# Moving start-up memsets and reordering the first loads in a one-core biased-attention kernel

## The chip, the cores and the metric

The kernel runs on one core of one Trainium2 chip. The metric is device time in microseconds (us) of one execution; lower is better. "Span" is the profiled part of an execution, in most runs some 1.8 us shorter than the time. Engines: PE is TensorE's matmul side (its weight loads are shown as PEld), DVE is VectorE, ACT is ScalarE, POOL is GpSimd, SP is SyncE.

## The reference

```
q, k, v: (4, 8, 1024, 64) float32;  bias: (1, 1, 1024, 1024) float32
scores = q @ k.T / sqrt(64) + bias
out    = softmax(scores) @ v            # (4, 8, 1024, 64) float32
```

The 32 heads are worked on in 16 pairs. The kernel computes S transposed on PE, exp on ACT, multiplies by exp(bias) on VectorE, and multiplies by V on PE. A column of ones beside V makes the same product deliver the row sums.

## The kernel before

The change touches only the start and two constants of the planner, a small model inside the kernel's builder that fixes each engine's instruction order. At the start, q and k of pair 0 arrive as float32 on the queues of SP and ACT, are cast to bf16, transposed on PE and copied into `qT0` and `kT0`. `mask` is used only later, by the copies of the other q tiles.

```python
nc.vector.memset(warm[:], 0.0)
nc.vector.memset(zeros[:], 0.0)
...                                                   # loads of kr0, qr0 and half the bias, issued by Pool
for t in range(2):
    nc.vector.memset(qT0[t*D:(t+1)*D, 1-t, :HQ], 0.0)
    for u in range(2):
        nc.vector.memset(mask[t*D:(t+1)*D, u, :], 1.0 if t == u else 0.0)
nc.gpsimd.memset(vall[:, :, :, D:D1], 1.0)            # the ones column: 256 elements per partition, 65 apart
load_v(0); load_qk(1)
...                                                   # second bias half, load_v(1), load_qk(2)
...                                                   # six warm-up matmuls wm on zeros
k_first(0, nc.scalar.copy, nc.scalar.copy, "xb")      # cast, 4 transposes, copy to kT0
c_a = q_first(0, "xa"); c_b = q_first(1, "xb")        # cast on VectorE, 4 transposes each
c_a(); c_b()                                          # copies to qT0 on VectorE
s_fill(0); s_exp(0)                                   # one S bank, first exponential
k_first(2, nc.vector.tensor_copy, nc.vector.tensor_copy, "xa")
s_fill(1); s_exp(1)                                   # two banks; all later groups have three
COLD = 10500; T0 = 6700.0                             # the planner's model of the cold clock and the start
```

The softmax here doesn't subtract the row's maximum and nothing guards it: scores larger than these inputs give would overflow.

Of the kernel before, what the change touches and what calls it, by code (L numbers as in the profile page):

```python
# [15 lines left out]
def kernel(  # L16
# [15 lines left out]
    nc = tc.nc  # L32
    B, H, S, D = q.shape
    P = 128
    NCH = S // P
    D1 = D + 1
    NP = B * H // 2
    scale = 1.0 / (D ** 0.5)
    HQ = S // 2
    QC = NCH // 2  # L40
# [5 lines left out]
    bf_ = bias.rearrange("a b (p c) k -> p (a b c) k", p=P)  # L46
# [12 lines left out]
    btraw = consts.tile([P, NCH, S], BF)  # L59
    eb = consts.tile([P, 2, NCH, HQ], BF)  # L60
    braw = consts.tile([P, 2, HQ], BF)
    mask = consts.tile([P, 2, HQ], BF)
    vall = consts.tile([P, 2 * NP, NCH, D1], BF)
# [8 lines left out]
    def load_qk(pr):  # L72
        qr = raw.tile([P, 2, NCH, D], BF, name="qr")
        kr = raw.tile([P, 2, NCH, D], BF, name="kr")
        nc.gpsimd.dma_start(out=kr.rearrange("p t c d -> p t (c d)"), in_=kf[pr])  # L75
        nc.gpsimd.dma_start(out=qr.rearrange("p t c d -> p t (c d)"), in_=qf[pr])  # L76
        raws[pr] = (qr, kr)

    def load_v(pr):
        for t in range(2):  # L80
            nc.gpsimd.dma_start(out=vall[:, 2 * pr + t, :, :D], in_=vf[pr, :, t])  # L81
# [34 lines left out]
    def e_at(b, n):  # L116
        if b // ET not in etiles:
            etiles[b // ET] = ep.tile([P, ET, HQ], BF, name="E")
        return etiles[b // ET][:, b % ET:b % ET + n, :]
# [3 lines left out]
    def s_fill(g):  # L123
        ps = ps_s.tile([P, 3, HQ], F32, tag="s", name="ps")
        open_ps[("S", g)] = ps
        for j, b in enumerate(slots[g]):
            pr, h, qh, kc = banks[b]
            qT, kT = trs[(pr, 0)], trs[(pr, 1)]
            nc.tensor.matmul(ps[:, j, :], kT[:, kc, :], qT[:, h, qh * HQ:(qh + 1) * HQ],  # L129
                             start=True, stop=b not in late_bias)  # L130
            if b in late_bias:
                nc.tensor.matmul(ps[:, j, :], ident[:], braw[:, late_bias[b], :], start=False, stop=True)

    def s_exp(g):
        n = len(slots[g])
        nc.scalar.activation(e_at(slots[g][0], n), open_ps.pop(("S", g))[:, :n, :], ACTF.Exp, scale=scale)  # L136
# [77 lines left out]
    with tc.manual_schedule():  # L214
# [13 lines left out]
        qT0 = kvp.tile([P, 2, NCH * P], BF, name="qT")  # L228
# [1 line left out]
        nc.gpsimd.dma_start(out=kr0[:, :, QC:, :].rearrange("p t c d -> p t (c d)"), in_=kf[0][:, :, QC * D:])  # L230
        nc.gpsimd.dma_start(out=qr0[:, :, QC:, :].rearrange("p t c d -> p t (c d)"), in_=qf[0][:, :, QC * D:])
        nc.gpsimd.dma_start(out=btraw[:, :QC, :], in_=bf_[:, :QC, :])
        for t in range(2):
            nc.vector.memset(qT0[t * D:(t + 1) * D, 1 - t, :HQ], 0.0)  # L234
            for u in range(2):
                nc.vector.memset(mask[t * D:(t + 1) * D, u, :], 1.0 if t == u else 0.0)  # L236
        nc.gpsimd.memset(vall[:, :, :, D:D1], 1.0)
        load_v(0)
        load_qk(1)
        nc.gpsimd.dma_start(out=btraw[:, QC:, :], in_=bf_[:, QC:, :])  # L240
        load_v(1)
        load_qk(2)

        wm = ps_s.tile([P, 3, HQ], F32, tag="s", name="wm")
        for i in range(6):
# [2 lines left out]
        def k_first(c0, eng_cast, eng_copy, tag):  # L248
            cs = slice(c0, c0 + 2)
            eng_cast(kr0[:, :, cs, :], k0f[:, :, cs, :])  # L250
            px = ps_x.tile([P, 2, P], BF, tag=tag, name="px")
            for c in range(2):
                for t in range(2):
                    nc.tensor.transpose(px[t * D:(t + 1) * D, c, :], kr0[:, t, c0 + c, :], ident[:])  # L254
            eng_copy(kT0[:, cs, :], px[:])
# [14 lines left out]
        s_fill(0)  # L270
        s_exp(0)
        k_first(2, nc.vector.tensor_copy, nc.vector.tensor_copy, "xa")
        for g in range(1, 2):
            s_fill(g)
            s_exp(g)



        COLD = 10500
        EXP, EXP0, QK, AV, TP = 427, 45, 216, 170, 350  # L280
        MUL, COPYQ, COPYK, EVAC, SEM = 600, 650, 420, 620, 80
        order = [("S", g) for g in range(2, NS)]
        for at, x in ((5, (0, 0)), (7, (0, 4)), (11, (1, 0)), (13, (1, 4))):
            order.insert(at, ("B",) + x)
        NO = len(order)
        T0 = 6700.0
        t_act, t_pe, t_dve = T0 + 700, T0, T0 + 500
        filled = []
        act_end = []
        x_free = {"xa": T0 + 500, "xb": T0}  # L290
        x_unit = {}
# [6 lines left out]
        pieces.append((NP, 0, 0))  # L298
        raw_at[NP] = (T0, T0)
        piece_end = {(0, 1, 0): T0, (0, 0, 0): T0}  # L300
        eb_at = {}
        exp_at = {0: T0, 1: T0 + 700, 2: T0 + 700}
        mul_at = {}
# [14 lines left out]
        def pe_cost(t, c):  # L318
            return c * 2 if t < COLD else c

# [4 lines left out]
        def act_end_of(i):  # L325
            if i < 0:
                return T0
            if i < len(act_end):
# [155 lines left out]
        while len(act_end) < NO or av_next < NB or dve_q:  # L484
# [11 lines left out]
            t, who = min(c)  # L496
# [53 lines left out]
```

## Time and profile before

Before the prediction: 252.03 us, median of 3 runs (251.59 to 252.09).

| Reading | Value | View |
|---|---|---|
| ACT busy | 239.0 of 249.9 us | page, part 1 |
| ACT from the first three-bank exponential to the last but a tail | busy all of 9.71 to 243.98 us | busy time by stretch |
| First q cast / second, same shape | 1.50 us / 0.28 us | timeline of VectorE |
| First, second, third, fourth exponential start | 6.77, 8.43, 9.71, 11.07 us | timeline of ACT |

ACT's timeline shows these four exponentials, the third and the fourth merged into one line. Each line gives start, duration, engine, line, operation and, in brackets, the engine's idle time just before it and what ended that:

```profile
6.77 0.60 ACT L136 ACTIVATE E<-ps 128x512 bf16<-128x512 f32 x1 [1.94 <-PE ps L129]
8.43 1.02 ACT L136 ACTIVATE E<-ps 128x1024 bf16<-128x1024 f32 x1 [1.06 <-PE ps L129]
9.71 2.81 ACT L136 ACTIVATE E<-ps 128x1536 bf16<-128x1536 f32 x2 [0.26 <-PE ps L129]
```

Part 1 of the page gives busy time, share of the span and number of instructions of each engine:

```profile
PE 228.8 (92%) x3097; PEld 141.1 (56%) x3152; DVE 221.2 (89%) x380; ACT 239.0 (96%) x180; POOL 54.0 (22%) x73
```

Busy time by stretch: the stretch, its length, then each engine's busy time in the order PE, PEld, DVE, ACT, POOL, then granted clock, DMA share and GB/s:

```profile
9.71:243.98 234.27, 219.90 (x3033) 137.33 (x3089) 213.16 (x360) 234.27 (x174) 45.30 (x58) 1.00 0.64 93
```

The fourth busy time, ACT's, equals the stretch: past 9.71 us ACT is never idle, so what comes earlier only moves the start of a queue of exponentials. The chain of waits says what set that start (start us, duration, what):

```profile
2.94 0.48 DVE mask L236
3.42 0.03 issue
3.46 1.51 DVE qr L258
...
5.01 0.65 PE px L261 x6
...
5.68 0.42 DVE qT L262
...
6.58 0.38 DVE kr L250
...
7.01 0.42 PE px L254 x3
7.43 2.26 PE ps L129 x5
```

The timeline (start, duration, engine, line, operation) puts Pool's memset right inside the slow cast; the line for DVE merges the two casts, 3.46 to 4.95 and 4.88 to 5.15 us:

```profile
3.46 1.70 DVE L258 CAST qr<-q0f 128x256 bf16<-128x256 f32 x2
3.54 1.26 POOL L237 MEMSET vall<- 128x256 bf16 x1
```

At PE's slow clock five S matmuls took 2.31 us, and VectorE was idle for 2.40 us ahead of the copy of K's second half (L102), which is the gap that the prediction counts on:

```profile
7.36 2.31 PE L129 MATMUL ps<-qT,kT 128*128 128x512 bf16 x5
10.16 0.42 DVE L102 COPY kT<-px 128x512 bf16<-128x512 bf16 x1 [2.40 <-PE px L89]
```

### The profile page before, as it was taken

The page shows a single profiled execution, that of the slowest core. Times are in us where ns is not written, and L with a number is a line of the kernel's source. Part 1 is how long each engine was busy: PE and PEld are TensorE (multiplying, and loading weights), DVE is VectorE, ACT ScalarE, POOL GpSimd, SP SyncE. Part 2 cuts the span into 40 slices and gives each one's busy share as a digit, 9 for nine tenths or more (in the row PEclk, how much of TensorE's full clock was granted, in tenths as well). Part 3 has the DMA queues.
Part 4 walks back from the last instruction along what each step waited for, and adds up shares of the span by engine and source line. Part 5 has one row for each costly group of instructions (what it writes and reads, how often), then busy time and mean ns, then how long its engine had stood idle before and what let it go on. Part 6 is the DMA issues. An engine that isn't in the chain of part 4 may idle for free.

```text
span 249.9 us, 7123 instructions
## 1 busy us (share of the span) xinstructions
PE 228.8 (92%) x3097; PEld 141.1 (56%) x3152; DVE 221.2 (89%) x380; ACT 239.0 (96%) x180; POOL 54.0 (22%) x73
## 2 busy tenths in 40 slices
PE   6969999999999999999999999999998999999893
PEld 2346655556566665565565555566665555665552
DVE  7229799899999998999999999999999999998884
ACT  3799999999999999999999999999999999999991
POOL 8753213054004132203150130416000000000000
PEclk9999999999999999999999999999999999999999
DMA  7999979369905987923958194949911102020112
GB/s 153 179 221 183 192 85 149 32 112 154 149 4 104 113 104 114 122 84 52 164 77 93 45 117 95 117 98 108 107 42 43 45 0 88 3 84 3 62 45 64
DMA packets 48175, 23.79 MB, mean 95 GB/s; under 512 B 34448, under 2 KB 44048, under 8 KB 47888
## 3 DMA queue, kind: packets, MB, share of 16 engines
q0 software_dynamic: 42272, 14.42, 52.8%
q1 hardware_dynamic: 5584, 8.72, 9.8%
q8 instruction: 24, 0.39, 0.6%
q10 hardware_dynamic: 288, 0.20, 0.3%
q14 instruction: 7, 0.06, 0.1%
HBM read 29.36 MB, written 8.39 MB: 151 GB/s over the span
## 4 chain that ended last, share of the span: by engine, by line
ACT 87%; PE 6%; DVE 4%; issue 2%; DVEq 0%; ACTq 0%
ACT E L136 84%; PE ps L129 4%; ACT eb L149 3%; PE po L186 1%; DVE mask L236 1%; DVE qr L258 1%; DVE E L155 1%; PE px L89 0%; DVE qT L262 0%; DVE qT L98 0%; PE px L261 0%; DVE E L158 0%; DVE qT L234 0%; DVE oall L206 0%; PE px L254 0%
## 5 line engine op out<-in xcount | busy, mean ns | idle before, releaser
L136 ACT ACTIVATE E<-ps 128x1536 bf16<-128x1536 f32 (+2 forms) x172 | 230.1, 1681 | 3.3 <-PE ps L129 3.3
L129 PE MATMUL ps<-qT,kT 128*128 128x512 bf16 x457 | 135.3, 381 | 11.3 <-ACT E L136 4.6
L186 PEld LDWEIGHTS <-E 128*128 128x128 bf16 x2048 | 82.9, 98 | 39.1 <-DVE E L158 2.7
L158 DVE TENSOR_TENSOR E<-E,eb 128x2048 bf16<-128x2048 bf16 x80 | 96.5, 1217 | 1.0 <-ACT E L136 0.5
L186 PE MATMUL po<-vall,E 128*128 128x65 bf16 x2048 | 92.5, 194 | 2.4 <-DVE E L161 0.8
L129 PEld LDWEIGHTS <-kT 128*128 128x128 bf16 x512 | 45.3, 97 | 43.0 <-issue 8.1
L161 DVE TENSOR_TENSOR E<-E,eb 128x1024 bf16<-128x1024 bf16 x88 | 58.2, 683 | 0.9 <-ACT E L136 0.6
L75 POOL DMA_DIRECT2D kr<-in_k_dram x15 | 10.5, 701 | 94.6 <-PE px L89 92.2
L81 POOL DMA_DIRECT2D vall<-in_v_dram x32 | 28.2, 884 | 6.1 <-DMA btraw<-in_bias_dram 4.0
L206 DVE TENSOR_TENSOR oall<-po,rs 128x256 f32<-128x256 f32 x63 | 26.7, 425 | 2.2
L98 DVE TENSOR_TENSOR qT<-px,mask 128x1024 bf16<-128x1024 bf16 x31 | 21.3, 688 | 4.6 <-PE px L89 4.0
L102 DVE COPY kT<-px 128x512 bf16<-128x512 bf16 x31 | 13.1, 422 | 10.2 <-PE px L89 10.0
L76 POOL DMA_DIRECT2D qr<-in_q_dram x15 | 10.8, 719 | 19.4 <-PE px L89 18.5
L196 DVE RECIPROCAL rs<-po 128x4 f32<-128x4 f32 x64 | 11.3, 177 | 3.4 <-PE po L186 3.1
L89 PEld LDWEIGHTS <-qr 128*64 128x64 bf16 x248 | 7.8, 109 | 9.4 <-issue 8.0
L89 PE MATMUL px<-ident,qr 128*64 128x128 bf16 x248 | 12.8, 225 | 0.1
L89 PE MATMUL px<-ident,kr 128*64 128x128 bf16 x248 | 12.9, 226 | 0.0
L89 PEld LDWEIGHTS <-kr 128*64 128x64 bf16 x248 | 8.0, 110 | 6.1 <-issue 4.2
L149 ACT ACTIVATE eb<-pb 128x2048 bf16<-128x2048 bf16 x4 | 7.5, 1882 | 0.0
L144 PE MATMUL pb<-ident,btraw 128*128 128x128 bf16 x64 | 4.6, 225 | 1.2 <-ACT eb L149 0.6
L144 PEld LDWEIGHTS <-btraw 128*128 128x128 bf16 x64 | 4.5, 146 | 1.6 <-issue 1.3
L155 DVE TENSOR_TENSOR E<-E,eb 128x1024 bf16<-128x1024 bf16 (+1 forms) x6 | 4.6, 775 | 0.6 <-ACT E L136 0.6
(35 smaller groups left out, 22.3 us busy)
## 6 DMA issues: line engine op xcount, KB each, us to landing
out_dram<-oall SPq DMA_DIRECT2D x30, 256.0 KB, 2.0
vall<-in_v_dram POOLq DMA_DIRECT2D x32, 128.0 KB, 5.6
kr<-in_k_dram POOLq DMA_DIRECT2D x15, 256.0 KB, 3.9
qr<-in_q_dram POOLq DMA_DIRECT2D x15, 256.0 KB, 5.3
btraw<-in_bias_dram POOLq DMA_DIRECT2D x2, 1024.0 KB, 10.7
out_dram<-oall SPq DMA_DIRECT2D x3, 128.0 KB, 1.7
k0f<-in_k_dram SPq DMA_DIRECT2D x2, 128.0 KB, 3.3
q0f<-in_q_dram ACTq DMA_DIRECT2D x1, 128.0 KB, 2.5
```

The lines of the kernel that those rows point to most:

```text
L81: nc.gpsimd.dma_start(out=vall[:, 2 * pr + t, :, :D], in_=vf[pr, :, t])
L89: nc.tensor.transpose(px[t * D:(t + 1) * D, c, :], src[:, t, half * QC + c, :], ident[:])
L98: nc.vector.tensor_tensor(dst[:, :, half * HQ:(half + 1) * HQ], px.rearrange("p c q -> p (c q)").unsqueeze(1).to_broadcast([P, 2, HQ]), ma ...
L102: nc.vector.tensor_copy(dst[:, half * QC:(half + 1) * QC, :], px[:])
L129: nc.tensor.matmul(ps[:, j, :], kT[:, kc, :], qT[:, h, qh * HQ:(qh + 1) * HQ], start=True, stop=b not in late_bias)
L136: nc.scalar.activation(e_at(slots[g][0], n), open_ps.pop(("S", g))[:, :n, :], ACTF.Exp, scale=scale)
L149: nc.scalar.activation(eb[:, qh, k0:k0 + 4, :], open_ps.pop(("B", qh, k0))[:, :4, :], ACTF.Exp)
L158: nc.vector.tensor_tensor(e, e, eb[:, qh, kc:kc + 2, :].unsqueeze(2).to_broadcast([P, 2, 2, HQ]), op=ALU.mult)
L161: nc.vector.tensor_tensor(e, e, eb[:, qh, kc:kc + 1, :].to_broadcast([P, n, HQ]), op=ALU.mult)
L186: nc.tensor.matmul(acc[:, i, :], e[:, 0, i * P:(i + 1) * P], vall[:, 2 * pr + h, kc, :], start=(kc == 0 and i == 0), stop=(kc == NCH - 1), ...
L196: nc.vector.reciprocal(rs[:], acc[:, :, D:D1])
L206: nc.vector.tensor_tensor(oall[:, c0:c0 + QC, :], acc[:, :, :D], rs[:].to_broadcast([P, QC, D]), op=ALU.mult)
```

## The change

The intent is to let the q casts start as soon as their data lands: the mask memsets and V's ones memset move on VectorE behind the second group's exponential, and pair 1's q and k are loaded ahead of V 0. V 0's loads now wait for the moved ones memset. Two planner constants follow the earlier start.

```diff
-        for t in range(2):
-            nc.vector.memset(qT0[t * D:(t + 1) * D, 1 - t, :HQ], 0.0)
-            for u in range(2):
-                nc.vector.memset(mask[t * D:(t + 1) * D, u, :], 1.0 if t == u else 0.0)
-        nc.gpsimd.memset(vall[:, :, :, D:D1], 1.0)
-        load_v(0)
+        nc.vector.memset(qT0[D:, 0, :HQ], 0.0)
+        nc.vector.memset(qT0[:D, 1, :HQ], 0.0)
         load_qk(1)
-        (second bias half, load_v(1), load_qk(2))
 ...
+        s_fill(1)
+        s_exp(1)
+        nc.vector.memset(vall[:, :, :, D:D1], 1.0)
+        for t in range(2):
+            for u in range(2):
+                nc.vector.memset(mask[t * D:(t + 1) * D, u, :], 1.0 if t == u else 0.0)
+        load_v(0)
+        (second bias half, load_v(1), load_qk(2))
-        COLD = 10500
+        COLD = 9500
-        T0 = 6700.0
+        T0 = 6200.0
```

More of the change, by code (lines that the diff above doesn't have):

```diff
@@ L232 @@
         nc.gpsimd.dma_start(out=btraw[:, :QC, :], in_=bf_[:, :QC, :])
-        for t in range(2):
-            nc.vector.memset(qT0[t * D:(t + 1) * D, 1 - t, :HQ], 0.0)
-            for u in range(2):
-                nc.vector.memset(mask[t * D:(t + 1) * D, u, :], 1.0 if t == u else 0.0)
-        nc.gpsimd.memset(vall[:, :, :, D:D1], 1.0)
-        load_v(0)
+        nc.vector.memset(qT0[D:, 0, :HQ], 0.0)
+        nc.vector.memset(qT0[:D, 1, :HQ], 0.0)
         load_qk(1)
-        nc.gpsimd.dma_start(out=btraw[:, QC:, :], in_=bf_[:, QC:, :])
-        load_v(1)
-        load_qk(2)
         wm = ps_s.tile([P, 3, HQ], F32, tag="s", name="wm")
@@ L272 @@
         k_first(2, nc.vector.tensor_copy, nc.vector.tensor_copy, "xa")
-        for g in range(1, 2):
-            s_fill(g)
-            s_exp(g)
-        COLD = 10500
+        s_fill(1)
[5 more added lines that the diff above has]
+        load_v(0)
+        nc.gpsimd.dma_start(out=btraw[:, QC:, :], in_=bf_[:, QC:, :])
+        load_v(1)
+        load_qk(2)
+        COLD = 9500
         EXP, EXP0, QK, AV, TP = 427, 45, 216, 170, 350
```

## The prediction

> **What bounds it now.** The page gives ACT 239.0 of 249.9 us busy. Busy time by stretch shows ACT busy 234.0 of the 234.0 us from 9.71 us (first three-bank exponential) to 243.98 us, and the wait list gives it only 3.3 us of waits for PE, all before 9.8 us. So the body is a queue of exponentials about 1.34 us apart, and a change can only move where that queue starts. The tail is not touched.
>
> **The start, from the timeline.** VectorE's memsets run from 0.81 to 3.42 us; then the first q cast (128x256) runs 3.46 to 4.96 us, 1.50 us, while the second, same shape, takes 0.275 us. Pool's memset of V's ones column runs 3.54 to 4.80 us, exactly inside the slow cast. [...] the cast ends 0.16 us after Pool's memset. The chain of waits runs through the mask memsets, this cast, px, qT copies, kr cast, px, five S matmuls, then ACT.
>
> **What the change does.**
> - Pool's memset (1.26 us) goes; the cast should fall from 1.50 to about 0.28 us.
> - Four mask memsets (1.51 us) leave the front of VectorE. Little gained: q's first load lands at 3.23 us (0.73 + 2.5); the cast started at 3.46.
> - The second q load lands at about 3.84 us (1.24 + 2.6), so the casts end near 3.53 and 4.13 us instead of 4.96 and 5.16.
> - Then PE is on K's first transposes until about 4.2 us, and the second q head's transposes need the PSUM buffer that ACT's kT copy frees at 4.83 us. Estimates: first qT copy 4.85 us (was 5.68), first exponential 5.95 (was 6.77), second qT copy 5.55 (was 6.13), kr cast 6.0 (was 6.58), the five matmuls from about 6.78 (was 7.36).
> - The moved memsets (1.51 us plus about 0.3 for V's ones) fall where VectorE idled 2.4 us, between the second kT copy (ends 7.76) and the next (10.16): free.
> - V 0's loads wait for the memset and start near 7.3 us instead of 5.10; first use is at 21.1 us. Pair 1's q and k come 3 us sooner than before. The second bias half is issued up to 1 us later and is needed at about 23.5 us. No cost.
>
> **How much survives.** About 0.6 us at the matmuls. PE's clock is the second limit: matmuls run 0.43 us apart until the trace's clock record turns at about 9.9 us. [...] if that stays at 9.9 us, the next transposes and three matmuls run more in the slow phase and give back about 0.2 us. The planner's new constants may reorder later work; I allow 0.3 us either way.
>
> **Prediction:** 251.5 us, a gain of about 0.5 us (0.2%); 80% range 250.7 to 252.1. Faster by over 2%: 0.01; within 2%: 0.98; slower by over 2%: 0.01.
>
> **What would show it.** First q cast near 0.28 us starting at 3.25 to 3.3 (waiting for its load); first qT copy near 4.85; first exponential near 5.95; first three-bank one near 9.1 to 9.3; ACT still gapless after that; last exponential about 0.5 us sooner; tail unchanged.
>
> **What would make it wrong.** The cast stays slow because Pool's load issues hold it up too; the PE clock turns much earlier or later; V 0 or the bias half comes late and ACT gets gaps at 16 to 30 us; the reordered plan costs ACT a stall.

The sum: about 0.6 us sooner at the five matmuls (7.36 to about 6.78 us), of which about 0.2 us is given back if the clock turns at 9.9 us. That leaves 0.4 to 0.6 us, put down as about 0.5 us (252.03 to 251.5 us), with 0.3 us either way for the planner.

## The result, and the profile after

251.66 us, median of 6 runs (251.22 to 252.19), against 252.06 us (251.59 to 252.77) for the kernel before in the same rounds. The ratio is 0.9984 with a 95% interval of 0.9963 to 1.0006: the same time at 2%, and not shown to be different at all.

Part 1 of the page after:

```profile
PE 229.8 (92%) x3152; PEld 141.3 (57%) x3152; DVE 220.4 (88%) x380; ACT 239.0 (96%) x180; POOL 52.6 (21%) x72
```

The q casts are no longer merged, and the first one waited for its load, as predicted. Timeline of VectorE after:

```profile
3.33 0.36 DVE L251 CAST qr<-q0f 128x256 bf16<-128x256 f32 x1 [1.42 <-DMA q0f<-in_q_dram]
3.93 0.45 DVE L251 CAST qr<-q0f 128x256 bf16<-128x256 f32 x1 [0.24 <-DMA q0f<-in_q_dram]
```

But the chain of waits after has a new stretch that was not there before; it ends at the fourth exponential:

```profile
6.53 0.29 DVE kT L248
6.82 0.88 issue
7.70 0.27 DVE vall L268
...
8.00 0.48 DVE mask L271
8.48 0.00 issue
8.48 0.27 DVE mask L271
8.76 0.09 issue
8.85 0.27 DVE mask L271
9.12 0.06 issue
9.18 0.48 DVE mask L271
9.66 0.03 issue
9.69 0.44 DVE kT L102
10.13 0.05 issue
10.18 0.40 PE ps L129
10.58 0.02 issue
10.60 1.45 ACT E L136
```

Read it backwards: the fourth exponential (10.60) waited for an S matmul (10.18), which waited for the copy of K's second half (9.69), which stood on VectorE behind the moved memsets. ACT's timeline shows the price in brackets, the idle time before an instruction:

```profile
5.77 0.60 ACT L136 ACTIVATE E<-ps 128x512 bf16<-128x512 f32 x1 [0.86 <-PE ps L129]
7.06 2.37 ACT L136 ACTIVATE E<-ps 128x1024 bf16<-128x1024 f32 x2 [0.70 <-PE ps L129]
10.60 2.79 ACT L136 ACTIVATE E<-ps 128x1536 bf16<-128x1536 f32 x2 [1.17 <-PE ps L129]
```

The third exponential came 1.73 us sooner (7.98 instead of 9.71 us), the fourth only 0.47 us. The last exponential ended 0.47 us sooner (244.40 instead of 244.87 us).

A second thing differs between these two traces: the clock record, that is, the moments at which PE's granted clock changes, which the trace keeps. The clock doubles at 9.85 us in the trace before and at 4.65 us in the trace after: matmuls of 128x512 in a row start 0.43 us apart ahead of it and 0.22 us apart behind it. The five S matmuls that took 2.31 us before took 1.25 us after:

```profile
6.42 1.25 PE L129 MATMUL ps<-qT,kT 128*128 128x512 bf16 x5
```

Part of the 1.73 us is therefore not the change's doing, and the experiments have to separate the two.

### The profile page after: what moved, and what is told of

The parts are those of the page before. It is cut to its first block, busy times and chain, and to the rows that moved or that the text cites. A ratio compares the mean times of both kernels' runs of the same rounds, so it can differ in the third digit from the quotient of the medians.

```text
span 249.4 us, 7171 instructions
## 1 busy us (share of the span) xinstructions
PE 229.8 (92%) x3152; PEld 141.3 (57%) x3152; DVE 220.4 (88%) x380; ACT 239.0 (96%) x180; POOL 52.6 (21%) x72
## 4 chain that ended last, share of the span: by engine, by line
ACT 77%; PE 13%; DVE 5%; issue 2%; DMA 1%; DVEq 0%; ACTq 0%
ACT E L136 74%; PE ps L129 10%; ACT eb L149 3%; PE po L186 2%; DVE E L161 2%; PE px L89 1%; DMA k0f<-in_k_dram 1%; DVE mask L271 1%; DVE E L155 1%; DVE qT L98 1%; DVE kT L102 0%; DVE oall L206 0%; PE px L247 0%; DVE rs L196 0%; DVE qT L255 0%
## 5 line engine op out<-in xcount | busy, mean ns | idle before, releaser
L129 PE MATMUL ps<-qT,kT 128*128 128x512 bf16 x512 | 138.2, 377 | 10.4 <-ACT E L136 4.7
L158 DVE TENSOR_TENSOR E<-E,eb 128x2048 bf16<-128x2048 bf16 x81 | 97.6, 1216 | 1.1 <-ACT E L136 0.7
L161 DVE TENSOR_TENSOR E<-E,eb 128x1024 bf16<-128x1024 bf16 x86 | 57.1, 683 | 6.7 <-ACT eb L149 5.6
```

The lines of the kernel that those rows point to most:

```text
L129: nc.tensor.matmul(ps[:, j, :], kT[:, kc, :], qT[:, h, qh * HQ:(qh + 1) * HQ], start=True, stop=b not in late_bias)
L158: nc.vector.tensor_tensor(e, e, eb[:, qh, kc:kc + 2, :].unsqueeze(2).to_broadcast([P, 2, 2, HQ]), op=ALU.mult)
L161: nc.vector.tensor_tensor(e, e, eb[:, qh, kc:kc + 1, :].to_broadcast([P, n, HQ]), op=ALU.mult)
```

## The experiments

Theory A: the slow cast waited for Pool's memset; taking it away frees the start, but the moved memsets hold up the kT copy that the fourth exponential needs, and that gives the gain back. Rivals: the mask memsets in front were the cost; or the load order or the planner constants carry the effect. Theory C came with the two clock records (9.85 and 4.65 us): the moment when PE's clock doubles depends on PE's idle gaps at the start, which was the assumption and not shown by a trace, and it moves the time by as much as the change does.

All kernels were correct. Each was timed in five rounds, and the runs of one group share the runs of the kernel before. The first four runs are group one, on one chip; the next four are group two and the last four group three, both on another chip and with eleven runs of the kernel before in common.

### 1. The changed kernel again

No edit.

> The changed kernel itself, repeated for a tighter ratio and a second trace. Both theories: ratio to the kernel before 0.997 to 1.000. If the TensorE clock turns later than the 4.65 us of the first trace (at about 8 or 9.9 us), the stall of ACT at the fourth exponential (1.17 us in the first trace) should shrink and the first exponentials should come later, so that the time stays about the same.

Measured: 251.65 us (251.55 to 251.95), ratio 0.9995 (0.9974 to 1.0016). The clock doubled at 9.73 us this time. First exponential 6.25 us, third 9.23, fourth 11.05: at nearly the clock of the trace before, the third exponential is 0.48 us sooner and the fourth 0.02 us. So at a like clock these two traces show no gain at the fourth exponential. The stall ahead of it was 0.37 us against 1.17 us in the first trace of this kernel, smaller as expected:

```profile
11.05 1.45 ACT L136 ACTIVATE E<-ps 128x1536 bf16<-128x1536 f32 x1 [0.37 <-PE ps L129]
```

The clock is not all that differs between two traces of one kernel. The first q load landed at 3.54 us here and at 3.31 us in the first trace, and over all 14 traces at 3.24 to 3.83 us.

### 2. Masks back in front

```diff
 nc.vector.memset(qT0[:D, 1, :HQ], 0.0)
+for t in range(2):
+    for u in range(2):
+        nc.vector.memset(mask[...], ...)     # and taken out behind s_exp(1)
```

> The changed kernel with the four mask memsets put back in front of the q casts; V's ones memset stays on VectorE behind the second kT copy. Theory A (the late mask memsets hold up the kT copy that the fourth exponential needs): first q cast starts near 3.46 us and still takes 0.3 to 0.4 us, first exponential within 0.15 us of the changed kernel's 5.77, no ACT wait over 0.4 us after the first three-bank exponential, and about 0.5 to 1.2 us faster than the changed kernel. Rival B (moving the masks away from the front is where the gain comes from, and the ACT wait comes from the clock or the plan): first exponential 0.5 us or more later, time equal to the kernel before or slower.

Measured: 251.38 us (249.99 to 252.29), ratio 0.9970 (0.9936 to 1.0005). Clock at 9.79 us. First cast 3.66 us, 0.29 us long; first exponential 6.28, third 9.25, fourth 10.74. Against run 1 at the same clock the start is unchanged, and the fourth exponential is 0.31 us sooner: putting the masks back costs nothing. Rival B, which wanted a later start, is out. In time the difference is not shown, because the runs spread over 2.3 us, and the expected 0.5 to 1.2 us was missed. The expectation of a start within 0.15 us of 5.77 us failed too, but not on the masks: run 1, with its masks late and the same clock, starts within 0.03 us of this run.

### 3. Only the masks moved

```diff
 for t in range(2):
     nc.vector.memset(qT0[...], 0.0)
-    for u in range(2):
-        nc.vector.memset(mask[...], ...)      # now behind s_exp(1); Pool's memset stays
```

> The kernel before with only the four mask memsets moved behind the second group's exponential; Pool's ones memset stays in front. Theory A [...]: the first q cast starts at 3.3 us, ahead of Pool's memset, and takes 0.3 to 0.4 us; Pool's memset starts late or the second cast is held by it until about 4.9 us. The time gains at most 0.4 us over the kernel before. Rival B (masks in front are the cost): both casts done by 4.4 us and the whole gain is there.

Measured: 251.68 us (250.87 to 252.24), ratio 0.9993 (0.9969 to 1.0016). First exponential 6.79 us, fourth 11.08 us: no gain. VectorE was free from 1.79 us on, yet the first cast still took 1.47 us. Timelines of VectorE and Pool in this run:

```profile
3.51 1.66 DVE L256 CAST qr<-q0f 128x256 bf16<-128x256 f32 x2 [1.72 <-DMA q0f<-in_q_dram]
3.54 1.29 POOL L235 MEMSET vall<- 128x256 bf16 x1
```

The masks in front were not the cost; Pool's memset was. One detail of the expectation failed: a cast that starts ahead of the memset was to take 0.3 to 0.4 us, but this cast's record starts 0.03 us ahead of the memset's and ends 0.15 us after it. (Pool was not idle then: its issue of the first bias load ran to 3.58 us.) The load landed too late for a real head start (cast at 3.51, expected 3.3), so the run does not show what happens when the two starts are well apart.

### 4. One word: the ones memset on VectorE, in its old place

```diff
-nc.gpsimd.memset(vall[:, :, :, D:D1], 1.0)
+nc.vector.memset(vall[:, :, :, D:D1], 1.0)
```

> The kernel before with one word changed: V's ones memset on VectorE instead of Pool, in its old place in front, masks in front, loads in the old order, old planner constants. Theory A: first q cast starts near 3.7 us and takes 0.3 to 0.4 us, first exponential at 5.7 to 6.0 us (6.77 before), no late memsets, so 0.6 to 1.5 us faster than the kernel before, and faster than the changed kernel by 0.3 to 1 us. Rival B (the gain needs the masks moved or pair 1 loaded early): no gain over 0.3 us.

Measured: 251.51 us (250.60 to 252.45), ratio 0.9986 (0.9958 to 1.0015): the expected gain was missed. First exponential 6.63 us, fourth 10.98. The memset's record is short, but it starts 1.00 us after the previous memset ended, with no semaphore, and the casts queue behind it (the first cast's record starts 0.11 us ahead of the memset's, but ends 0.12 us after it). VectorE's timeline in this run:

```profile
2.61 0.81 DVE L236 MEMSET mask<- 64x256 uint32 x2
4.31 0.50 DVE L258 CAST qr<-q0f 128x256 bf16<-128x256 f32 x1 [0.88 <-DMA q0f<-in_q_dram]
4.42 0.27 DVE L237 MEMSET vall<- 128x256 bf16 x1
```

The same pause, 0.88 us, stands ahead of this memset in the changed kernel (the "issue" line of the chain at 6.82 us). So the ones memset occupies VectorE for 1.15 us and not for the 0.27 us of its record.

### 5. The ones memset split, 48 elements in front and 208 late

```diff
 (masks in front, as in run 2)
+nc.vector.memset(vall[:, :6, :, D:D1], 1.0)       # pairs 0 to 2
 ...
+nc.vector.memset(vall[:, 6:, :, D:D1], 1.0)       # behind the first masked q copy
```

> The kernel with masks in front, with V's ones memset on VectorE split: 48 of 256 elements per partition (pairs 0 to 2) in front behind the masks, 208 behind the first masked q copy, where VectorE idles for 5 us. In all four traces with this memset on VectorE its record shows 0.27 us but it starts 0.9 to 1.0 us after its predecessor ended, without a semaphore. If the pause is per element (strided 2-byte writes cost about 4.5 ns each), the small one pauses about 0.2 us and the large one about 0.7 us; if it is fixed, both pause 0.9 us. With the clock turning near 9.8 us: time within 0.3 us of masks in front, since its fourth exponential was only 0.14 us late there.

Measured: 250.36 us (249.92 to 252.46), ratio 0.9945 (0.9907 to 0.9983). The median beat the expectation by 1 us, but the trace of this run, with its clock at 10.43 us, is an ordinary one (fourth exponential 11.08 us, 249.8 us span), and five of the six runs were of spans 248.1 to 248.8. This may be clock luck, but that is not shown: only the slowest of the six was traced, its first q load landed later (3.83 us) than in any other trace, and run 7, the same kernel with dummies, is not faster. The split gives the pause: 48 elements paused 0.24 us here (0.13 us in run 9), and 208 elements paused 0.70 us here and in runs 7 and 9. Pause plus record is 0.93 us for 208 and 1.15 us for 256, 4.5 ns an element both times; the 48 elements of run 9 took 0.22 us, 4.6 ns each. In these runs the cost is per element, not fixed.

### 6. The changed kernel with dummy matmuls in PE's gaps

```diff
+filler(384)                       # matmul on zeros into the warm-up tile
 k_first(0, ...)
 c_a = q_first(0, "xa")
+filler(256)
 c_b = q_first(1, "xb")
+filler(128)
 ...
 s_exp(0)
+filler(512)
 k_first(2, ...)
```

> The changed kernel with four dummy matmul blocks (384, 256, 128, 512 columns of zeros) in PE's gaps at 3.8, 4.9, 5.5 and 6.1 us. Theory C [...]: the clock turns at 4 to 7.2 us in the trace instead of 9.8. Theory A then says that the late mask memsets catch ACT: the fourth exponential late by 0.8 to 1.3 us, so that the gain stays under 0.5 us against the changed kernel. Rival (the clock does not depend on those gaps): turn at 9.7 to 9.9 us, time unchanged or up to 0.4 us slower.

Measured: 251.78 us (251.45 to 252.91), ratio 0.9996 (0.9964 to 1.0029). The clock doubled at 5.04 us, within the expected 4 to 7.2 us. The start was fast, and the stall came in full. VectorE, then ACT:

```profile
6.82 0.29 DVE L253 COPY kT<-px 128x256 bf16<-128x256 bf16 x1 [0.40 <-PE px L252]
7.99 0.27 DVE L276 MEMSET vall<- 128x256 bf16 x1 [0.88 <-issue]
8.29 1.67 DVE L279 MEMSET mask<- 64x512 bf16 x4
9.98 0.42 DVE L102 COPY kT<-px 128x512 bf16<-128x512 bf16 x1
```

```profile
7.35 2.36 ACT L136 ACTIVATE E<-ps 128x1024 bf16<-128x1024 f32 x2 [0.71 <-PE ps L129]
10.89 1.45 ACT L136 ACTIVATE E<-ps 128x1536 bf16<-128x1536 f32 x1 [1.18 <-PE ps L129]
```

The early clock helps the changed kernel little (fourth exponential 10.89 us against 11.05 us in run 1, and the times are not told apart): VectorE is now what the fourth exponential waits for, and its memsets, pauses included, took 2.84 us here and 2.83 us in run 1.

### 7. Masks in front, ones split, dummies

Edits of runs 2, 5 and 6 together.

> Masks in front, ones memset split, and the same dummy matmuls. Theories A and C together: clock turns at 4 to 7.2 us, no exponential late by over 0.3 us, and about 249.9 to 250.6 us, 1.3 to 2 us faster than the kernel before and 0.8 us or more faster than the changed kernel with the same dummies. Rival: same as masks in front, 251.4 us.

Measured: 250.80 us (250.55 to 251.00), ratio 0.9952 (0.9923 to 0.9981); the time was expected at 249.9 to 250.6 and missed that narrowly. Clock at 4.99 us, third exponential 8.68, fourth 10.01, on time. The runs spread over 0.45 us, against 2.7 us for the kernel before in the same group; but run 1, without dummies, spread over 0.40 us and the other runs with dummies over 0.65 to 1.8 us, so a smaller spread is not shown to come from the dummies. Nor is a shorter time: run 5, the same kernel without them, has 250.36 us and a ratio of 0.9945. What the trace shows is VectorE's gap ahead of the copy of K's second half with nothing put into it. At this clock it is 1.24 us, not 2.40:

```profile
8.75 0.42 DVE L102 COPY kT<-px 128x512 bf16<-128x512 bf16 x1 [1.24 <-PE px L89]
```

The kr cast took 0.67 us while Pool issued V 0's loads (4.96 to 6.73 us).

### 8. The kernel before with dummies

> The kernel before with the same dummy matmuls; Pool's memset still in front. Theory A: first q cast stays at 1.5 us, first exponential at 6.6 to 6.9 us. Theory C: clock turns early [...]; then up to 1 us faster than the kernel before. If the clock stays at 9.8 us: no gain.

Measured: 251.94 us (250.74 to 252.50), ratio 0.9985 (0.9946 to 1.0023). Clock at 9.66 us, first cast 1.22 us (it ended 0.15 us after Pool's memset, as in the kernel before), first exponential 7.23 us, later than expected (its first q load landed at 3.72 us, against 3.24 us in the kernel before). In this trace the dummies alone did not bring the clock forward; the slow cast that PE's transposes wait for was still there, but that it is the reason is not shown. They bought nothing.

### 9. As run 7, small ones memset behind the second kT copy

> Masks in front, dummies on PE, V's ones memset split: 48 elements behind the second kT copy, 208 behind the first masked q copy. V 0's loads wait for the small memset, so Pool issues nothing from 5.0 to about 7.1 us. If Pool's issuing of loads slows VectorE's casts (kr cast 0.67 us with V 0 issued at 5 us, 0.29 us where Pool was idle), the kr cast falls back to 0.29 us and the third exponential comes at 8.1 to 8.4 us instead of 8.68; no exponential late by over 0.3 us; 0.3 to 0.5 us faster than with the small memset in front (250.8 us), so 250.3 to 250.6. If the slow cast had another cause: 250.8.

Measured: 250.59 us (250.25 to 250.90), ratio 0.9945 (0.9912 to 0.9977). The kr cast fell to 0.29 us, and the fourth exponential started at 9.93 us. VectorE's timeline of run 7 first, then that of this run:

```profile
6.15 0.67 DVE L252 CAST kr<-k0f 128x256 bf16<-128x256 f32 x1
```

```profile
6.46 0.29 DVE L251 CAST kr<-k0f 128x256 bf16<-128x256 f32 x1
```

In this trace the clock doubled at 6.29 us, later than in run 7, so the third exponential (8.60 us) missed its 8.1 to 8.4. Runs 7 and 9 are not told apart in time, so the expected 0.3 to 0.5 us is not shown. With run 5 this kernel has the lowest ratio, and its slowest run (250.90 us) is below the fastest of the changed kernel (251.22 us in 12 runs).

### 10. As run 6, but masks in front

> As the changed kernel with dummies, but masks in front; the whole ones memset (1.15 us with its pause) stays late. If the mask memsets (1.67 us) are what held the kT copy, the fourth exponential is late by under 0.3 us against 1.28 us and the time is 0.8 to 1.2 us below the changed kernel with dummies (251.78 us). If the ones memset is as guilty, it is still late by 0.5 us or more. The clock must turn at 4 to 7 us for this to count.

Measured: 250.67 us (250.52 to 251.39), ratio 0.9952 (0.9922 to 0.9982). Clock at 6.85 us. VectorE and ACT:

```profile
8.52 0.27 DVE L279 MEMSET vall<- 128x256 bf16 x1 [0.89 <-issue]
8.87 0.42 DVE L102 COPY kT<-px 128x512 bf16<-128x512 bf16 x1
```

```profile
7.87 5.05 ACT L136 ACTIVATE E<-ps 128x1024 bf16<-128x1024 f32 x4 [0.52 <-PE ps L129]
```

Four exponentials run without a gap, and the time is 1.1 us below run 6 (medians of two groups on one chip; the six runs of one and the six of the other do not overlap). The only difference to run 6 is where the masks stand: the fourth exponential is at 10.12 instead of 10.89 us although the clock came later. The mask memsets, at the wrong place, are what took the gain; the ones memset alone, late, fits into the gap of 1.24 us.

### 11. As run 9, old planner constants

```diff
-COLD = 9500;  T0 = 6200.0
+COLD = 10500; T0 = 6700.0
```

> The first kernel of this group with the old planner constants (start 6700, cold limit 10500). If the constants matter little, the time is within 0.25 us of it and ACT has no new gap; PE's order still differs in many places. Rival: the new constants carry part of the gain, then 0.3 us or more slower.

Measured: 250.74 us (250.42 to 251.31), ratio 0.9951 (0.9921 to 0.9981). The fourth exponential to the end of the last took 233.88 us against 233.80 us in run 9. The 0.08 us more lie ahead of one bias exponential (24.07 us), whose half of the bias landed at 22.80 us, against 21.93 us in run 9. That the constants did this is not shown, and the times are not told apart.

### 12. As run 9, V 0 loaded ahead of pair 1

```diff
-load_qk(1)                     # early
 ...
 load_v(0)
+load_qk(1)
```

> The first kernel of this group with V 0 loaded ahead of pair 1's q and k, the old load order. If the load order matters not at all, the same time within 0.25 us, and pair 1's first transposes at 16 to 17.5 us wait for nothing. Rival: pair 1 lands late and ACT gets a gap of 0.5 us or more at 17 to 22 us.

Measured: 251.10 us (250.16 to 251.95), ratio 0.9954 (0.9920 to 0.9988). In the trace the second half of the bias landed late, at 23.05 us. ACT's part of the timeline shows the bias exponential waiting for its transposes:

```profile
24.34 1.88 ACT L149 ACTIVATE eb<-pb 128x2048 bf16<-128x2048 bf16 x1 [0.39 <-PE pb L144]
```

That exponential came 0.49 us later than ACT's pace in run 9, where the bias landed at 21.93 us. So in this trace the load order does carry something: the bias half was issued at 10.73 us, behind the loads of V 0 (from 7.58 us) and pair 1 (from 9.33 us), and landed 12.32 us later. Why it landed later than in run 9 was not tested. Its trace also ended with a tail of 6.34 us after the last exponential, 5.0 us in all others: the last two stores landed 2.98 and 2.94 us after their issue, against 1.57 and 1.60 us in run 9. Why stays open. The times do not separate this run from run 9.

### All traces side by side

| Kernel | Clock doubles, us | First exponential | Third to fourth | Fourth starts | Fourth to end of last |
|---|---|---|---|---|---|
| before | 9.85 | 6.77 | 1.36 | 11.07 | 233.80 |
| after | 4.65 | 5.77 | 2.62 | 10.60 | 233.80 |
| 1 after again | 9.73 | 6.25 | 1.82 | 11.05 | 233.79 |
| 2 masks in front | 9.79 | 6.28 | 1.48 | 10.74 | 233.79 |
| 3 only masks moved | 9.72 | 6.79 | 1.35 | 11.08 | 233.78 |
| 4 one word | 9.79 | 6.63 | 1.38 | 10.98 | 233.78 |
| 5 ones split | 10.43 | 6.53 | 1.49 | 11.08 | 233.78 |
| 6 after, dummies | 5.04 | 6.04 | 2.62 | 10.89 | 233.79 |
| 7 split, dummies | 4.99 | 6.07 | 1.33 | 10.01 | 233.80 |
| 8 before, dummies | 9.66 | 7.23 | 1.35 | 11.39 | 233.80 |
| 9 split late, dummies | 6.29 | 6.55 | 1.33 | 9.93 | 233.80 |
| 10 masks in front, dummies | 6.85 | 6.76 | 1.33 | 10.12 | 233.80 |
| 11 as 9, old constants | 5.00 | 6.13 | 1.33 | 9.69 | 233.88 |
| 12 as 9, V 0 first | 4.20 | 5.99 | 1.33 | 9.55 | 234.29 |

Third to fourth is 1.33 to 1.38 us when nothing stalls, and 1.48 and 1.49 us in runs 2 and 5. The last column is the finding that makes everything else simple: once the fourth exponential has started, the rest takes the same time, whatever was changed ahead of it. Only runs 11 and 12 differ (233.88 and 234.29 us), where a bias exponential came late.

## Why the prediction was right or wrong

- **The time.** 251.5 us predicted, 251.66 us measured: inside the range. That is luck more than proof. The range (250.7 to 252.1 us) also holds the kernel before (252.06 us), and a gain is not shown. In the trace the fourth exponential did move by 0.47 us, close to the predicted gain, but as 1.73 us won at an early clock less a stall that the prediction had excluded. At a like clock (before and run 1) it moved by 0.02 us, and run 1's time ratio is 0.9995.
- **What bounds it: right.** ACT's queue fixed the body at 233.8 us, and the tail did not move.
- **The slow cast: right.** It fell from 1.50 to 0.36 us once Pool's memset was gone. With Pool's memset in place it ended 0.16 us after that memset in the kernel before and 0.15 us after it in runs 3 and 8, with the masks in front (before and run 8) or without (run 3). Why is not shown, nor what happens when the two starts are well apart. The new cast took 0.36 us, against the 0.28 us predicted, and ended 0.12 us after Pool's issue of a bias load (see the last section); that the issue is the cause is not shown.
- **The estimates up to the kr cast: right in the first trace.** First qT copy 4.89 us (4.85 predicted), second 5.38 (5.55), kr cast 5.84 (6.0), first exponential 5.77 (5.95). But they were made for a late clock, and this trace had an early one. In run 1, where the clock stood as assumed, the same steps came 0.16 to 0.30 us later than predicted (first qT copy 5.08, second 5.71, kr cast 6.17, first exponential 6.25 us), and the third exponential at 9.23 us (9.1 to 9.3 predicted).
- **V 0 and the bias: right in the conclusion.** V 0's loads started at 8.27 us (7.3 predicted) and the second bias half was issued 1.8 us later than before (up to 1 predicted), but ACT got no gap from either.
- **The step that failed** reads: "The moved memsets (1.51 us plus about 0.3 for V's ones) fall where VectorE idled 2.4 us, between the second kT copy (ends 7.76) and the next (10.16): free." It failed twice. The memsets were mis-sized: they took 2.84 us, not 1.8. The ones memset took 1.15 us, not 0.3, because 0.88 us of it stands in the profile as an unexplained pause, and the masks took 1.67 us with the small gaps between them. And the gap is not fixed. The earlier start alone left it as it was (2.40 us before; 2.52 us in run 2, at nearly the same clock, with the time of the ones memset counted in), but once the clock had doubled by 6.9 us it was 1.24 us (runs 7, 9 and 10), because PE's work that ends the gap was done sooner (five S matmuls in 1.25 us instead of 2.31). The memsets occupied VectorE from 6.82 to 9.66 us, and ACT was idle for 1.17 us, against the prediction of "ACT still gapless after that".
- **The clock: only half right.** A give-back of 0.2 us was allowed for a clock at 9.9 us; the trace turned at 4.65 us. In all 14 traces the clock's rise and its fall at the end lie 238.93 us (seven traces) or 242.35 us (seven traces) apart, which is 70 or 71 times their difference of 3.413 us, and with dummies in PE's gaps the rise came between 4.2 and 6.9 us in all six kernels without Pool's memset in front, but not in run 8 (9.66 us). Without dummies and without Pool's memset in front the rise came at 4.65 us in one trace (after) and at 9.73 to 10.43 us in four (runs 1, 2, 4 and 5). What sets its moment, and why the two lengths are such multiples, no run here shows. That an early clock pays is seen in traces (fourth exponential at 10.12 us in run 10 and 10.74 us in run 2), but no pair of kernels with and without dummies (runs 6 and 1, 7 and 5, 8 and before, 10 and 2) shows it in the times.
- **What follows for the spread.** In groups one and two the kernel before had spans of 248.9 to 249.0 us in 4 of 22 runs and 249.8 to 250.5 us in the rest. That those four had the early clock is possible but not shown, as its one trace is of the late kind; run 12's trace shows another source, stores at the end that landed 1.3 us later. A spread of this size hides a change worth half a microsecond.

## What to carry to other kernels

Work is only free in another engine's idle time if that idle time will still be there after the change: recompute the gap for the state in which the instruction that ends it comes earliest (here at PE's early clock: 1.24 us instead of 2.40), and measure what the moved work takes with the pauses ahead of it (2.84 us here, not the 1.8 us expected). Put start-up work that depends on nothing where the engine waits for its first load (VectorE waited 1.42 us for it in the trace after), rather than behind the first critical results; here the masks cost nothing in front (runs 2 and 10). When a saturated queue follows, compare traces by the start of that queue, at equal clock, before believing a difference in the times.

## What else the traces show

- The memset of V's ones, 2-byte elements 65 apart on 128 partitions, cost 4.5 ns an element (256 in 1.15 us, 208 in 0.93 us), against 0.95 ns for the adjacent ones of a mask memset on 64 partitions (512 in 0.485 us). Other strides were not tried, so what makes the difference is not shown.
- The record of that memset shows only 0.27 us and the rest stands as a pause without a semaphore ahead of it (0.87 to 0.89 us in five traces, 1.00 us in run 4). Sums of busy time miss it.
- In a kernel tuned this far, the clock at the start can be the size of the changes under test: with zero matmuls in PE's start-up gaps the clock doubled at 6.85 instead of 9.79 us and the fourth exponential started 0.62 us sooner (run 10 against run 2, one trace each), 0.25% of the span.
- VectorE's casts and Pool's issues of loads: leaving aside the casts that ran beside Pool's memset, 15 of VectorE's casts at the start of the 14 traces had been under way for more than 0.1 us when an issue of Pool's ended; all 15 ended 0.09 to 0.12 us after it, having taken 0.30 to 0.67 us (in run 7 the kr cast ran from 6.15 to 6.82 us, the issue to 6.73 us). Casts that met no issue, or were over before it ended, took 0.27 to 0.29 us unless a memset of VectorE's own stood ahead (run 8: cast over at 7.34 us, issue at 7.57 us). This is read from the order of events, and that the issue holds the cast is not shown; the one run that moved an issue, run 9, moved the small memset too.
